# Causal attention in a Mamba-2/MLA decoder trunk: score banks in pairs, low probabilities side by side, work only behind a tile's last chunk

## The chip, the cores and the metric

The kernel runs on one core of a Trainium2 chip. The metric is the device time of one execution in microseconds. The profile is of one such execution; its engines are PE (TensorE matmuls; PEld are its weight loads), DVE (VectorE), ACT (ScalarE), POOL (GpSimd) and SP (SyncE, which only issues DMAs here).

## The reference

Two layers are computed on 2048 rows of width 1024: a Mamba-2 mixer, then multi-head latent attention with 16 heads, and a final norm. The change lies in the attention alone:

```
for i in range(S // Q_BLOCK):                      # blocks of 128 queries
    s = einsum(q_nope, k_nope) + einsum(q_rope, k_rope)   # 64 + 32 = 96 deep
    mask = (q0 + local)[:, None] >= arange(kv_len)[None, :]
    p = softmax(where(mask, s * scale, -inf))
    outs.append(einsum('bhqk,bkhd->bqhd', p, v[:, :kv_len]))
```

All is float32. The kernel keeps that accuracy by splitting each operand into a high and a low half, so that one product is three matmuls (high by high, high by low, low by high).

## The kernel before, in words

The program is recorded stage by stage: Mamba-2 (`mamba`), the projections of the attention (`mla`), the attention (`attention`, `heads`), and gate, output projection and norm (`back`). PE's order in the attention is the order in which the code is written (`manual_schedule`); on DVE, ACT, POOL and SP a scheduler that works ahead of time fixes the order, and on the chip each engine takes its instructions strictly in it.

`heads` goes through 16 heads, each with four query blocks of 512 (`qb` 0 to 3, called q0 to q3 here), each with four **tiles** of 128 queries (`j` 0 to 3). A tile's scores against its 128 to 2048 keys are computed in **chunks** of up to 512 keys, one PSUM bank each.

For each tile, `scores` does this:

- three matmuls for each chunk (`mm3`, L85 to L87), and in the last chunk one more that adds the causal mask (L1062, or L1060 in the first tile of a head);
- a maximum over each chunk on DVE (L1063, tile `mx`), then the negated maximum over the chunks (L1067, `nm`);
- an exponential of each chunk on ACT (L1075, tile `Pr`), which needs `nm`, sums its row on the way, and is what sets the chunk's bank free; these are recorded between the chunks of the next tile;
- the sum over the chunks on DVE (L1079).

The probabilities then have to be turned, 128 by 128, for the product with the values. A **unit** is one block of 128 keys against a query block. Its turning (`turn`, called T) is up to four transposes on PE into a bank (L1090); ACT then writes the high half as float16 (L123, called the copy here), and DVE subtracts it to get the low half (L124, called the low half). Its product (`values`, called V) is one matmul with the high half and one with the low half (L1100, L1101), both against 128 columns: 64 of the high half of the values, 64 of the low. They add up over the query block in one bank `O`, which `finish` copies out (L1107) and sends to memory.

Scores run about a query block ahead of T and V. How many of these stand behind which chunk is written out by hand in the table `CREDIT`: its entry for block, tile and chunk is a string of T and V, done in that order behind the chunk. For q3 it spreads them over the chunks, such as `("TV", "V", "", "TVTVT")` in the last tile. PSUM has eight banks of 2 KB in a partition: four with the tag `mm` for scores, four with the tag `tr` for the turned blocks and `O`; the first 18 chunks of the stage alternate between both. The buffers `Pr` are 24 of 512 columns.

POOL and SP carry the DMAs of the stage: POOL loads keys, values and queries of the next head and adds the second half of `O` in memory (L1113); SP stores the first half (L1109).

Of the kernel before, what the change touches and what calls it, by code (L numbers as in the profile page):

```python
# [20 lines left out]
P = 128  # L21
# [12 lines left out]
WSP = 6  # L34
AHEAD = 10
UPS = (0, 1, 2, 3, 6, 4, 5)
NP = 24
SZ = 4
EV0 = ['big', 'Xp', 'big', 'Sp', 'wsp']
EV1 = ['big', 'yT', 'Xp', 'big', 'Sp']  # L40
LAG = 20
DEPTH = 2
CREDIT = (
    (("VT",), ("TV",), ("VT",), ("TV",)),
    (("", "VTVT"), ("", "TTVV"), ("", "TTVV"), ("", "TTVV")),
    (("TT", "", "VVTV"), ("TV", "", "VTTV"), ("TV", "", "TTVV"), ("TTV", "", "TVV")),
    (("T", "", "", "VVTTVTV"), ("T", "V", "", "VTTVTV"), ("T", "V", "V", "TVTTV"), ("TV", "V", "", "TVTVT")),
)
MAGIC = 12582912.0
PSCALE = 32768.0  # L50
TINY = 2.0 ** -100
# [17 lines left out]
class Net:  # L69
# [5 lines left out]
    def name(self, s):  # L75
        self.n += 1
        return f"{s}_{self.n}"

    def t(self, pool, tag, shape, dt=F32, bufs=None):
        return pool.tile(shape, dt, name=self.name(tag), tag=tag, bufs=bufs)  # L80


# [234 lines left out]
    def layers(self):  # L317
        with ExitStack() as ctx:
            tc = self.tc
            early = ExitStack()  # L320
# [691 lines left out]
    def attention(self):  # L1012
        with ExitStack() as ctx:
            self.wo = self.tail.enter_context(self.tc.tile_pool(name="wo", bufs=1, side="right", reuse_waits="tile"))
            self.wraw = []
            sp = ctx.enter_context(self.tc.tile_pool(name="asp", bufs=2, reuse_waits="tile"))
            with self.tc.manual_schedule(engines={mybir.EngineType.PE}):
                self.heads(sp)

    def heads(self, sp):  # L1020
        nc, v = self.nc, self.nc.vector
        begun = []
        keys, vals, quer = self.keys, self.vals, self.quer

        def cuts(kv):

            out, at = [], 0
            while at < kv:
                w = min(TB, kv - at)
                if kv - at == TB + P:  # L1030
                    w = 384
                out.append((at, max(w, 256)))
                at += w
            return out

        def scores(h, qb, st):
# [8 lines left out]
            for j in range(4):  # L1045
                qs = slice(j * P, (j + 1) * P)
                parts = cuts(qb * TB + (j + 1) * P)
                nb = len(parts)
                mx = self.t(sp, "mx", [P, 4], bufs=4)
                banks = []  # L1050
                for n, (c0, w) in enumerate(parts):
                    if late:
                        late.pop(0)()
                    begun.append(0)
                    s = self.t(self.pp, "tr" if len(begun) <= 18 and len(begun) % 2 == 1 else "mm", [P, TB], bufs=4)
                    ks = slice(c0, c0 + w)
                    self.mm3(s[:, :w], Q[:, 0, qs], Q[:, 1, qs], K[:, 0, ks], K[:, 1, ks], True, n < nb - 1)
                    if n == nb - 1:
                        if qb == j == 0:
                            nc.tensor.matmul(s[:, 0:w], self.idb, self.mk, start=False, stop=True)  # L1060
                        else:
                            nc.tensor.matmul(s[:, w - P:w], self.idb, self.mk[:, 0:P], start=False, stop=True)  # L1062
                    v.tensor_reduce(mx[:, n:n + 1], s[:, :w], AX.X, ALU.max)  # L1063
# [3 lines left out]
                v.tensor_reduce(nm, mx[:, :nb], AX.X, ALU.max, negate=True)  # L1067
                p = {}
                sm = self.t(sp, "sm", [P, 4], bufs=4)
                st["P"].append(p)  # L1070

                def exp(n, j=j, nb=nb, parts=parts, banks=banks, nm=nm, p=p, sm=sm):
                    s, w = banks[n]
                    x = self.t(sp, "Pr", [P, TB], bufs=NP)
                    nc.scalar.activation(x[:, :w], s[:, :w], AF.Exp, bias=nm, accum_out=sm[:, n:n + 1])  # L1075
                    for c in range(0, w, P):
                        p[(parts[n][0] + c) // P] = x[:, c:c + P]
                    if n == nb - 1:
                        v.tensor_reduce(sums[h][:, 4 * qb + j:4 * qb + j + 1], sm[:, :nb], AX.X, ALU.add)  # L1079

                late += [lambda n=n, f=exp: f(n) for n in range(nb)]
            for f in late:
# [2 lines left out]
        def turn(h, qb, kb, st):  # L1085
# [3 lines left out]
            for j in range(jj, 4):  # L1089
                nc.tensor.transpose(pt[:, j * P:(j + 1) * P], st["P"][j][kb], self.ident)  # L1090
            c = slice(jj * P, TB)
            u = self.t(sp, "PTs", [P, 2, TB], F16, bufs=5)
            self.pair16(u[:, 0, c], u[:, 1, c], pt[:, c], PSCALE)
            return u[:, :, c], c

        def values(h, qb, kb, st, u, c):
            if kb == 0:
                st["O"] = self.t(self.pp, "tr", [P, TB], bufs=4)
            nk = 4 * qb + 4
            nc.tensor.matmul(st["O"][:, c], vals[h][:, kb, :], u[:, 0], start=kb == 0, stop=False)  # L1100
            nc.tensor.matmul(st["O"][:, c], vals[h][:, kb, :], u[:, 1], start=False, stop=kb == nk - 1)  # L1101
            if kb == nk - 1:
                finish(h, qb, st)

        def finish(h, qb, st):
            o = self.t(sp, "Os", [P, TB], bufs=3)
# [18 lines left out]
        states = [{"P": []} for _ in jobs]  # L1125
        sums = {}
        def ahead():
            for n, (h, qb) in enumerate(jobs):
# [5 lines left out]
        held = []  # L1134

        def work(what):

            if what == "T" and units:
                a = units.pop(0)
                held.append((a, turn(*a)))  # L1140
            elif what == "V" and held and (len(held) > DEPTH or not units):
                a, (u, c) = held.pop(0)
                values(*a, u, c)

        step = 0
        for credit in ahead():
            step += 1
            if step > LAG:
                for what in credit:
                    work(what)  # L1150
        while units or held:
            work("T")
            work("V")


    def back(self):
        nc, a, v, hp = self.nc, self.a, self.nc.vector, self.hp
        with ExitStack() as ctx:
            sp = ctx.enter_context(self.tc.tile_pool(name="bsp", bufs=2, reuse_waits="tile"))
            self.sp = sp  # L1160
            us = self.t(self.sm, "us", [P, KD])
            nc.sync.dma_start(us, self.us_d.rearrange("(k p) -> p k", p=P))
# [187 lines left out]
```

## Time and profile before

| what | value |
|---|---|
| runs | 3198.4, 3201.06 and 3201.17 us, median 3201.06 |
| the profiled execution's own time | 3198.45 us |
| its span, from first to last instruction | 3196.7 us |
| granted TensorE clock, mean | 0.997 |
| PE, DVE, ACT, POOL busy | 3098.7, 2371.4, 2016.2, 658.8 us |
| first and last score mask of the attention (L1060, L1062) | 2084.9 and 2988.2 us |

The profile's tables are read like this. A group's row names line, engine, operation, output and input tiles, their shapes and the count; then the busy time, the mean duration of one in ns, and the idle time just before them with what ended it. A row of the timeline gives the start in us from the span's beginning, the duration in us, and in brackets the idle time before and its releaser. Matmuls are pipelined: their durations overlap, so the time that one costs is read from the distance of two starts. A row of stretches gives the bounds, the length, and the busy time of each engine asked for with its instructions in brackets, then the granted clock.

### The profile page before, as it was taken

Reading aid. Unit: us, or ns where it says so; the run is one execution under the profiler, and the core shown is the slowest. Engines: PE = TensorE matmul, PEld = TensorE weight load, DVE = VectorE, ACT = ScalarE, POOL = GpSimd, SP = SyncE. Lnnn points to the kernel's source line nnn. Section 1 sums busy time; section 2 is a strip of 40 time slices with the busy share of each in tenths; the row PEclk is TensorE's granted clock in tenths of the full one; section 3 lists DMA queues with packets and bytes.
Section 4 is the critical chain, followed back from the end, with each engine's and each line's share of the span. In section 5 each row is a group of like instructions: output and inputs, shape, how many; then the busy total and the mean of one; then the engine's idle time right before and its main releaser. Section 6 shows DMA issues by size and latency. Waiting matters only on the chain.

```text
span 3196.7 us, 51296 instructions
## 1 busy us (share of the span) xinstructions
PE 3098.7 (97%) x17735; PEld 2244.6 (70%) x17735; DVE 2371.4 (74%) x4786; ACT 2016.2 (63%) x5027; POOL 658.8 (21%) x927
## 2 busy tenths in 40 slices
PE   8999999999999999999999999999999999999998
PEld 6787654556655566665878888877777777777777
DVE  6888787777666666766766665678888888888675
ACT  7888576665555464555646554477877778778522
POOL 1222232321122211312111211322222122222100
PEclk9999999999999999999999999999999999999999
DMA  5443656554343345534486655843434434444494
GB/s 176 131 128 125 225 190 230 189 183 154 133 166 125 120 143 185 172 120 138 128 273 222 222 191 192 266 111 77 92 79 85 86 77 92 81 97 104 99 274 158
DMA packets 213236, 482.52 MB, mean 151 GB/s; under 512 B 28976, under 2 KB 62768, under 8 KB 211536
## 3 DMA queue, kind: packets, MB, share of 16 engines
q1 hardware_dynamic: 160672, 316.02, 31.2%
q0 software_dynamic: 52304, 163.22, 18.9%
q8 instruction: 140, 2.29, 0.3%
q14 instruction: 120, 0.98, 0.1%
HBM read 347.02 MB, written 132.12 MB: 150 GB/s over the span
## 4 chain that ended last, share of the span: by engine, by line
PE 65%; DVE 8%; ACT 6%; DMA 5%; issue 2%; POOL 1%; SPq 0%; ACTq 0%; DVEq 0%; POOLq 0%
PE mm L85 13%; PE mm L86 12%; PE mm L87 12%; PE tr L1090 6%; PE tr L1100 3%; PE tr L1101 3%; PE tr L86 3%; PE tr L87 3%; PE tr L85 3%; DVE cacc L495 2%; DMA wraw<-in_ssm_w_in_dram 2%; PE tr L699 1%; ACT Pr L1075 1%; DMA os<-ri_d 1%; DMA big<-cumT 1%
## 5 line engine op out<-in xcount | busy, mean ns | idle before, releaser
L124 DVE SCALAR_TENSOR_TENSOR PTs<-tr,PTs 128x512 f16<-128x512 f32 (+3 forms) x640 | 375.0, 607 | 92.4 <-ACT PTs L123 86.6
L123 ACT ACTIVATE PTs<-tr 128x512 f16<-128x512 f32 (+3 forms) x640 | 328.5, 541 | 141.1 <-PE tr L1090 140.7
L1063 DVE TENSOR_REDUCE mx<-mm 128x1 f32<-128x512 f32 (+2 forms) x631 | 375.7, 608 | 46.8 <-PE mm L87 44.3
L1075 ACT ACTIVATE Pr<-mm,nm 128x512 f32<-128x512 f32 (+2 forms) x631 | 395.7, 636 | 23.1 <-DVE nm L1067 21.4
L1090 PE MATMUL tr<-pack,Pr 128*128 128x128 f32 x2176 | 317.6, 273 | 1.4 <-ACT Os L1107 1.3
L85 PE MATMUL mm<-xT,wsp 128*128 128x512 f16 (+1 forms) x800 | 310.3, 388 | 0.0
L85 PE MATMUL mm<-K,xT 96*128 96x512 f32 (+2 forms) x639 | 287.0, 449 | 23.3 <-ACT Pr L1075 21.9
L86 PE MATMUL mm<-xT,wsp 128*128 128x512 f16 (+1 forms) x800 | 307.6, 384 | 0.0
L87 PE MATMUL mm<-xT,wsp 128*128 128x512 f16 (+1 forms) x800 | 307.3, 385 | 0.2 <-DVE wsp L116 0.2
L1090 PEld LDWEIGHTS tr<-pack,Pr 128*128 128x128 f32 x2176 | 253.2, 141 | 49.8 <-ACT Os L1107 2.1
L495 DVE SCALAR_TENSOR_TENSOR cacc<-craw,pack,cacc 128x512 f32<-128x512 f32 x288 | 219.9, 785 | 27.6 <-ACT cacc L493 25.5
L85 PE MATMUL mm<-wsp,xT 128*128 128x512 f16 (+2 forms) x640 | 235.9, 369 | 3.1 <-ACT craw L489 3.0
L86 PE MATMUL mm<-wsp,xT 128*128 128x512 f16 (+2 forms) x640 | 234.2, 366 | 0.0
L87 PE MATMUL mm<-wsp,xT 128*128 128x512 f16 (+2 forms) x640 | 233.6, 366 | 0.0
L86 PE MATMUL mm<-K,xT 96*128 96x512 f32 (+2 forms) x639 | 231.8, 363 | 0.0
L87 PE MATMUL mm<-K,xT 96*128 96x512 f32 (+2 forms) x639 | 231.2, 362 | 0.0
L1100 PE MATMUL tr<-PTs,xT 128*128 128x512 f16 (+3 forms) x640 | 222.2, 349 | 0.1
L1101 PE MATMUL tr<-PTs,xT 128*128 128x512 f16 (+3 forms) x640 | 219.7, 347 | 0.0
L85 PE MATMUL mm<-wsp,yT 128*128 128x512 f32 x512 | 208.9, 408 | 8.4 <-DMA wsp<-wo_d 4.5
L692 ACT ACTIVATE Xw<-tr,d_wend 128x64 f32<-128x64 f32 x512 | 112.0, 329 | 155.8 <-DVE y L689 127.6
L86 PE MATMUL mm<-wsp,yT 128*128 128x512 f32 x512 | 204.1, 399 | 0.0
L87 PE MATMUL mm<-wsp,yT 128*128 128x512 f32 x512 | 203.9, 398 | 0.0
(421 smaller groups left out, 7417.9 us busy)
## 6 DMA issues: line engine op xcount, KB each, us to landing
wsp<-wo_d SPq DMA_DIRECT2D x96, 512.0 KB, 3.6
wraw<-in_ssm_w_in_dram SPq DMA_DIRECT2D x128, 256.0 KB, 3.0
big<-cumT SPq DMA_DIRECT2D x64, 512.0 KB, 4.7
wsp<-w_d SPq DMA_DIRECT2D x64, 512.0 KB, 3.7
wo_d<-wsp POOLq DMA_DIRECT2D x32, 512.0 KB, 4.6
w_d<-wsp POOLq DMA_DIRECT2D x32, 512.0 KB, 5.0
xT<-qn_d POOLq DMA_DIRECT2D x64, 256.0 KB, 4.6
K<-kn_d POOLq DMA_DIRECT2D x15, 1024.0 KB, 8.4
```

Of the source, the lines that this page charges most:

```text
L85: mm(out, l_hi, r_hi, start=start, stop=False)
L86: mm(out, l_hi, r_lo, start=False, stop=False)
L87: mm(out, l_lo, r_hi, start=False, stop=stop)
L123: self.nc.scalar.activation(hi, src, AF.Copy, scale=scale)
L124: self.nc.vector.scalar_tensor_tensor(lo, src, scale, hi, ALU.mult, ALU.subtract)
L495: nc.vector.scalar_tensor_tensor(acc, raw[:, k:k + TB], wk[k], acc, ALU.mult, ALU.add)
L692: act(Xw[:, hc], px[:, hc], AF.Copy, scale=wend[:, h0 + h:h0 + h + 1])
L1063: v.tensor_reduce(mx[:, n:n + 1], s[:, :w], AX.X, ALU.max)
L1075: nc.scalar.activation(x[:, :w], s[:, :w], AF.Exp, bias=nm, accum_out=sm[:, n:n + 1])
L1090: nc.tensor.transpose(pt[:, j * P:(j + 1) * P], st["P"][j][kb], self.ident)
L1100: nc.tensor.matmul(st["O"][:, c], vals[h][:, kb, :], u[:, 0], start=kb == 0, stop=False)
L1101: nc.tensor.matmul(st["O"][:, c], vals[h][:, kb, :], u[:, 1], start=False, stop=kb == nk - 1)
```

## The change

Four things change in the attention.

1. **Scores by pairs of banks.** A tile's keys are cut into pieces of up to 1024 (two chunks of equal width side by side in a pair of banks). There are two such pairs, in a pool of their own; the four `tr` banks stay. One maximum (L1072 in the changed kernel) and one exponential (L1084) take a whole pair, and the first 18 chunks no longer use `tr`. `Pr` becomes 14 buffers of 1024.
2. **All T and V behind the tile's last chunk.** `CREDIT` goes; `BEHIND` gives one string for each query block, done behind the last chunk of each of its tiles.
3. **Low probabilities side by side.** `values` does the high half alone (L1112). The low halves are kept (`PTl`, 18 buffers) until the query block is through; `lows` then multiplies them all in a row (L1123), against the 64 columns of high values only, even units into partitions 0 to 63 of `O` and odd ones into 64 to 127. The product of low probabilities and low values is left out.
4. **A row sum of one piece** is copied by POOL (L1090 of the changed kernel) and not reduced by DVE: 8 of 16 tiles of a head.

```diff
+BEHIND = ("TV", "TVTV", "TTVVTV", "TTVVTVTV")
...
-                out.append((at, max(w, 256)))
+                out.append((at, 1, max(w, 256)) if w <= TB else (at, 2, w // 2))
...
-                for n, (c0, w) in enumerate(parts):
...
-                    s = self.t(self.pp, "tr" if len(begun) <= 18 and len(begun) % 2 == 1 else "mm", [P, TB], bufs=4)
...
-                    v.tensor_reduce(mx[:, n:n + 1], s[:, :w], AX.X, ALU.max)
-                    banks.append((s, w))
-                    yield CREDIT[qb][j][n]
+                for c0, m, w in parts:
+                    for i in range(m):
...
+                        if i == 0:
+                            pair = self.t(self.pm, "pair", [P, 2, TB], bufs=2)
+                            banks.append(pair[:, :m, :w])
...
+                        if i == m - 1:
+                            v.tensor_reduce(mx[:, len(banks) - 1:len(banks)], banks[-1], AX.XY, ALU.max)
+                        yield BEHIND[qb] if end else "", end
                 nm = self.t(sp, "nm", [P, 1], bufs=4)
                 v.tensor_reduce(nm, mx[:, :nb], AX.X, ALU.max, negate=True)
...
-                    nc.scalar.activation(x[:, :w], s[:, :w], AF.Exp, bias=nm, accum_out=sm[:, n:n + 1])
+                    nc.scalar.activation(x.rearrange("p (m w) -> p m w", m=m), banks[n], AF.Exp, bias=nm,
+                                         accum_out=sm[:, n:n + 1])
...
+                        if nb == 1:
+                            nc.gpsimd.tensor_copy(sums[h][:, 4 * qb + j:4 * qb + j + 1], sm[:, 0:1])
...
-            nc.tensor.matmul(st["O"][:, c], vals[h][:, kb, :], u[:, 1], start=False, stop=kb == nk - 1)
+        def lows(h, qb, st):
+            nk = len(st["lo"])
+            for i, (kb, l, c) in enumerate(st["lo"]):
+                d = slice(i % 2 * 64, i % 2 * 64 + 64)
+                nc.tensor.matmul(st["O"][d, c], vals[h][:, kb, 0:64], l, start=False, stop=i >= nk - 2)
+            finish(h, qb, st)
```

What stands in a row is shown at three places of one head (the ninth), with the line numbers of the kernel that the rows are from.

First DVE, at the end of the last tile of q3 and so of the head's scores. The change, from the tile's first maximum to its negated maximum `nm`:

```order
L1072 TENSOR_REDUCE mx_27929<-pair_27932 128x1
L1092 TENSOR_REDUCE sum_27221<-sm_27928 128x1
L1072 TENSOR_REDUCE mx_27929<-pair_27943 128x1
L127 SCALAR_TENSOR_TENSOR PTl_27958<-tr_27952,PTh_27957 128x512
L127 SCALAR_TENSOR_TENSOR PTl_27967<-tr_27961,PTh_27966 128x512
L127 SCALAR_TENSOR_TENSOR PTl_27978<-tr_27972,PTh_27977 128x512
L127 SCALAR_TENSOR_TENSOR PTl_27987<-tr_27982,PTh_27986 128x384
L1076 TENSOR_REDUCE nm_27991<-mx_27929 128x1
```

Before, the same tile:

```order
L1063 TENSOR_REDUCE mx_28140<-mm_28143 128x1
L124 SCALAR_TENSOR_TENSOR PTs_28153<-tr_28148,PTs_28153 128x512
L1063 TENSOR_REDUCE mx_28140<-mm_28160 128x1
L1063 TENSOR_REDUCE mx_28140<-mm_28169 128x1
L1079 TENSOR_REDUCE sum_27421<-sm_28139 128x1
L1063 TENSOR_REDUCE mx_28140<-mm_28177 128x1
L1067 TENSOR_REDUCE nm_28211<-mx_28140 128x1
L124 SCALAR_TENSOR_TENSOR PTs_28188<-tr_28183,PTs_28188 128x512
```

The negated maximum moved from ahead of the low halves to behind four of them, which belong to the T behind this tile's own last chunk. In a head of the changed kernel low halves stand between last maximum and `nm` in nine of 16 tiles: one in the second and fourth tile of q0, two in the second and fourth of q1, three in the second to fourth of q2, two in the second of q3, four in its last. Before it is five tiles, with one or two each: the first and third of q0, the first two of q1, the first of q3.

Then ACT at the same tile. The change, from the last exponential of the tile before to the first of the next head:

```order
L1084 ACTIVATE Pr_27936,sm_27928<-pair_27864,nm_27926 128x896
L126 ACTIVATE PTh_27957<-tr_27952 128x512
L126 ACTIVATE PTh_27966<-tr_27961 128x512
L126 ACTIVATE PTh_27977<-tr_27972 128x512
L126 ACTIVATE PTh_27986<-tr_27982 128x384
L1084 ACTIVATE Pr_27994,sm_27993<-pair_27932,nm_27991 128x1024
L1084 ACTIVATE Pr_27996,sm_27993<-pair_27943,nm_27991 128x1024
```

Before, the same stretch:

```order
L1075 ACTIVATE Pr_28174,sm_28139<-mm_28102,nm_28137 128x384
L123 ACTIVATE PTs_28188<-tr_28183 128x512
L1075 ACTIVATE Pr_28214,sm_28213<-mm_28143,nm_28211 128x512
L123 ACTIVATE PTs_28198<-tr_28193 128x512
L1075 ACTIVATE Pr_28216,sm_28213<-mm_28160,nm_28211 128x512
L123 ACTIVATE PTs_28208<-tr_28203 128x512
L1075 ACTIVATE Pr_28218,sm_28213<-mm_28169,nm_28211 128x512
L1075 ACTIVATE Pr_28220,sm_28213<-mm_28177,nm_28211 128x512
```

Copies and exponentials took turns; now four copies stand ahead of the tile's first exponential.

Last PE, at the end of the first tile of q3. The change, from its mask to the next T: the four low products of the same head's q0 block, 64 columns of weights each.

```order
L1070 MATMUL pair_27729<-mk,idb 128x128
L1123 LDWEIGHTS xT_26703
L1123 MATMUL tr_27656<-PTl_27608,xT_26703 64x512
L1123 LDWEIGHTS xT_26703
L1123 MATMUL tr_27656<-PTl_27616,xT_26703 64x384
L1123 LDWEIGHTS xT_26703
L1123 MATMUL tr_27656<-PTl_27625,xT_26703 64x256
L1123 LDWEIGHTS xT_26703
L1123 MATMUL tr_27656<-PTl_27684,xT_26703 64x128
L1103 MATMUL tr_27746<-pack,Pr_27368 128x128
```

Before, the same place: high and low products of the last two units of that block.

```order
L1062 MATMUL mm_27947<-mk,idb 128x128
L1100 LDWEIGHTS xT_26882
L1100 MATMUL tr_27904<-PTs_27858,xT_26882 128x256
L1101 LDWEIGHTS xT_26882
L1101 MATMUL tr_27904<-PTs_27858,xT_26882 128x256
L1100 LDWEIGHTS xT_26882
L1100 MATMUL tr_27904<-PTs_27863,xT_26882 128x128
L1101 LDWEIGHTS xT_26882
L1101 MATMUL tr_27904<-PTs_27863,xT_26882 128x128
L1090 MATMUL tr_27961<-pack,Pr_27556 128x128
```

The low products left the rows of the high ones and stand together at the end of the query block. Outside the attention no engine's order changes up to the stage's first scores, and the number of DMAs is the same.

More of the change, by code (lines that the diff above doesn't have):

```diff
@@ L36 @@
 UPS = (0, 1, 2, 3, 6, 4, 5)
-NP = 24
+NP = 14
+NL = 18
 SZ = 4
@@ L77, in name, with banks @@
         return f"{s}_{self.n}"
+    def banks(self, ctx):
+        self.pm = ctx.enter_context(self.tc.tile_pool(name="pm", bufs=4, space=PSUM, reuse_waits="tile"))
     def t(self, pool, tag, shape, dt=F32, bufs=None):
+        if tag == "mm":
+            pool = self.pm
         return pool.tile(shape, dt, name=self.name(tag), tag=tag, bufs=bufs)
@@ L319, in layers @@
             tc = self.tc
+            self.banks(ctx)
             early = ExitStack()
@@ L1098, in values @@
                 st["O"] = self.t(self.pp, "tr", [P, TB], bufs=4)
[L1099 to L1103, printed above, removed]
+            nc.tensor.matmul(st["O"][:, c], vals[h][:, kb, :], u[0], start=kb == 0, stop=False)
+            st["lo"].append((kb, u[1], c))
+            if kb == 4 * qb + 3:
+                owed.append((h, qb, st))
+        def lows(h, qb, st):
[4 more added lines that the diff above has]
+            finish(h, qb, st)
         def finish(h, qb, st):
@@ L1142, in work @@
                 a, (u, c) = held.pop(0)
+                if a[2] == 0 and owed:
+                    lows(*owed.pop())
                 values(*a, u, c)
         step = 0
-        for credit in ahead():
+        for credit, end in ahead():
             step += 1
             if step > LAG:
+                if end and owed:
+                    lows(*owed.pop())
                 for what in credit:
@@ L1159, in back @@
             sp = ctx.enter_context(self.tc.tile_pool(name="bsp", bufs=2, reuse_waits="tile"))
+            self.banks(ctx)
             self.sp = sp
```

60 lines of the change are left out of this document (29 added, 31 removed).

## The prediction

> **What bounds the kernel now.** I read the shares of busy time on the page first, then two stretches: one head of the attention (from one first-tile mask to the next), and the opening of the attention. Columns of a stretch: bounds, length, busy PE, PEld, DVE, ACT, POOL with instructions, clock, DMA share, GB/s. The row of the first-tile mask gives the head's period.
>
> ```profile
> PE 3098.7 (97%) x17735; PEld 2244.6 (70%) x17735; DVE 2371.4 (74%) x4786; ACT 2016.2 (63%) x5027; POOL 658.8 (21%) x927
> 2473.81:2530.86 57.05, 55.77 (x356) 42.83 (x355) 48.07 (x115) 45.27 (x126) 12.07 (x20) 1.00 0.41 84
> 2086.00:2101.00 15.00, 14.05 (x78) 10.81 (x77) 12.99 (x44) 12.06 (x39) 8.13 (x14) 1.00 0.98 199
> L1060 PE MATMUL mm<-mk,idb x15: 283/283/284, 2131.7 to 2931.5; 128*128 128x256 bf16 x15
> ```
>
> PE is the bound: it idles 57.05 - 55.77 = 1.3 us of a head, and (2931.5 - 2131.7) / 14 = 57.1 us is the period throughout. DVE and ACT have 9 and 12 us to spare in a head. So work taken off PE counts in full as long as PE finds no new wait, and every new wait of PE counts in full too. What PE waits for when it does wait is seen in the one long wait of a head, in the second tile of q3 (timeline, DVE, ACT and PE rows picked):
>
> ```profile
> 2508.62 0.23 PE L1062 MATMUL mm<-mk,idb 128*128 128x128 bf16 x1
> ...
> 2509.21 0.88 DVE L1063 TENSOR_REDUCE mx<-mm 128x1 f32<-128x384 f32 x2
> ...
> 2509.72 1.08 ACT L123 ACTIVATE PTs<-tr 128x512 f16<-128x512 f32 x2
> ...
> 2510.35 1.29 DVE L124 SCALAR_TENSOR_TENSOR PTs<-tr,PTs 128x512 f16<-128x512 f32 x2 [0.26 <-ACT PTs L123]
> ...
> 2511.55 0.15 DVE L1067 TENSOR_REDUCE nm<-mx 128x1 f32<-128x4 f32 x1
> ...
> 2511.74 0.69 ACT L1075 ACTIVATE Pr<-mm,nm 128x512 f32<-128x512 f32 x1
> ...
> 2512.57 0.50 PE L85 MATMUL mm<-K,xT 96*128 96x512 f32 x1 [1.21 <-ACT Pr L1075]
> ```
>
> The chain runs: last score, maxima, two low halves, negated maximum, exponential, next score. This is one of the tiles where two low halves stand ahead of `nm`, and PE stands 1.21 us. `nm` ends 0.04 us before the exponential starts, and the score starts 0.14 us after the exponential ends (2511.74 + 0.69 = 2512.43). I use these two lags below. Two copies start 1.08 - 0.60 = 0.48 us apart, two low halves 1.29 - 0.69 = 0.60.
>
> **What PE saves.** The low products go from 128 columns of weights to 64, two at a time. Starts of PE rows give what each step costs now:
>
> ```profile
> 2903.30 0.39 PE L86 MATMUL mm<-K,xT 96*128 96x512 f32 x1
> 2903.53 0.40 PE L87 MATMUL mm<-K,xT 96*128 96x512 f32 x1
> 2903.76 0.23 PE L1062 MATMUL mm<-mk,idb 128*128 128x128 bf16 x1
> 2903.83 0.61 PE L1090 MATMUL tr<-pack,Pr 128*128 128x128 f32 x4
> 2904.27 0.38 PE L1100 MATMUL tr<-PTs,xT 128*128 128x512 f16 x1
> 2904.49 0.38 PE L1101 MATMUL tr<-PTs,xT 128*128 128x512 f16 x1
> 2904.71 0.33 PE L1100 MATMUL tr<-PTs,xT 128*128 128x384 f16 x1
> 2904.87 0.33 PE L1101 MATMUL tr<-PTs,xT 128*128 128x384 f16 x1
> ```
>
> A score matmul costs 0.23 us for 512 columns (0.69 for a chunk), the mask 0.07, a T 0.44 (0.11 for each transpose), a product 0.22 for 512 columns, 0.16 for 384, and so about 0.11 and 0.06 for 256 and 128. A head has 28 low products of 512 and four each of 384, 256 and 128: 28 x 0.22 + 4 x 0.33 = 7.5 us. If two halves of the array really run at once, a query block costs its even units alone, 4.0 us in a head: **3.5 us saved**. The trace has matmuls of 64 columns into two halves, at L699 (two groups with the mean of one in ns, then rows of the timeline):
>
> ```profile
> L668 PE MATMUL tr<-BC,BC 128*128 128x128 f32 x128 | 24.7, 275 | 0.0
> L699 PE MATMUL tr<-Xd,big 128*64 128x64 f32 x2048 | 73.8, 225 | 11.2 <-DVE big L678 7.4 <-DVE Xd L686 2.9 <-issue 0.8
> ...
> 801.97 0.39 PE L668 MATMUL tr<-BC,BC 128*128 128x128 f32 x2
> ...
> 85.46 0.40 PE L87 MATMUL mm<-xT,wsp 128*128 128x512 f32 x1
> 85.78 1.15 PE L699 MATMUL tr<-Xd,big 128*64 128x64 f32 x32
> 86.86 0.50 PE L85 MATMUL mm<-xT,wsp 128*128 128x512 f32 x1
> 87.20 0.39 PE L86 MATMUL mm<-xT,wsp 128*128 128x512 f32 x1
> ```
>
> 32 rows take 1.15 us; less 0.225 for the last, 31 steps of 0.03 us. Full-width rows of 128 columns at L668 stand 0.115 apart (0.39 less 0.275), so serial ones of 64 columns would stand 0.06 apart: they do overlap. That is float32 and short; for long float16 rows the saving lies between 0 and 3.5 us, and I take 3.5. Going in and out of the halves is not free: L699 starts 0.32 us after its forerunner instead of 0.23, and L85 behind it starts 0.12 late and is followed 0.34 later instead of 0.23, together 0.31 us. Four query blocks make 1.2 us. PE's work in a head: 55.8 - 3.5 + 1.2 = **53.5 us**. The other parts move little on PE: the same chunks, masks and transposes.
>
> **What the pairs cost.** Groups over the attention, with the mean of one in ns:
>
> ```profile
> L1075 ACT ACTIVATE Pr<-mm,nm 128x512 f32<-128x512 f32 x392 | 268.9, 695 | 16.8 <-DVE nm L1067 15.2
> L1075 ACT ACTIVATE Pr<-mm,nm 128x256 f32<-128x256 f32 x122 | 60.9, 499 | 0.0
> L123 ACT ACTIVATE PTs<-tr 128x512 f16<-128x512 f32 x440 | 253.7, 600 | 85.8 <-PE tr L1090 85.3
> L1063 DVE TENSOR_REDUCE mx<-mm 128x1 f32<-128x512 f32 x390 | 265.7, 686 | 45.6 <-PE mm L87 43.7 <-PE mm L1062 0.3
> L1063 DVE TENSOR_REDUCE mx<-mm 128x1 f32<-128x256 f32 x122 | 50.7, 415 | 0.3 <-PE mm L1062 0.3
> L124 DVE SCALAR_TENSOR_TENSOR PTs<-tr,PTs 128x512 f16<-128x512 f32 x440 | 294.9, 688 | 75.2 <-ACT PTs L123 69.5
> L124 DVE SCALAR_TENSOR_TENSOR PTs<-tr,PTs 128x384 f16<-128x384 f32 x63 | 34.8, 553 | 2.5 <-ACT PTs L123 2.3
> L124 DVE SCALAR_TENSOR_TENSOR PTs<-tr,PTs 128x128 f16<-128x128 f32 x63 | 17.9, 283 | 4.1 <-ACT PTs L123 4.1
> ```
>
> No row shows a pair. From 256 to 512 columns a maximum gains 0.27 us and an exponential 0.20, so 1024 columns cost 0.69 + 2 x 0.27 = 1.23 and 0.70 + 2 x 0.20 = 1.09 us. Both cost at least what one bank does (0.69 and 0.70); I take the slopes. DVE and ACT issue fewer instructions and gain some us in a head, but neither is the bound, so that gives nothing. POOL's copies of row sums cost nothing as long as POOL, busy 12 of 57 us, is at most four tiles late: only then would an exponential wait for the buffer. `O` lives on until the low products are through, and so do the values; with one bank for it three are left for T, as now, and the next values have most of a head to arrive: nothing for both, but a T that waits for a bank would show it.
>
> In q2 and q3 a tile now fills both pairs, so its first exponential must end before the next tile may start, and it needs the maximum of the second pair, which ends last. PE meanwhile has only the T and V of `BEHIND`. Time from the end of the tile's mask:
>
> - *Last tile of q3* (two pairs of 1024). Second maximum 0.04 to 1.27. PE runs four T and four V with 15 transposes: 15 x 0.11 + 4 x 0.22 = 2.5 us. The fourth T ends at about 2.5, its copy at 3.0; DVE's four low halves end at 3.7, `nm` at 3.75, the exponential runs 3.8 to 4.9, the next score starts at 5.0. **Wait 2.5**, and 0.2 for the second pair.
> - *Last tile of q2* (1024 and 512). Second maximum, behind the first, until 1.1; low halves of 128, 512, 512 (the third copy lands at 2.0) until 2.7; `nm` 2.8; exponential to 3.9; score at 4.1. PE's work: nine transposes 1.0, V of 384, 256 and 128 0.3: 1.3 us. **Wait 2.8**.
> - *Second tile of q2* (1024 and 256). Maximum until 1.2, low halves of 384, 256, 128 until 2.2, `nm` 2.3, exponential to 3.4, score at 3.6; PE's work 6 x 0.11 + 3 x 0.22 = 1.3. **Wait 2.2**.
> - *Last tile of q1* (one pair, two low halves ahead): its exponential ends at 3.8; PE has 1.3 of T and V and one pair of 1.2. **Wait 1.4**.
> - In the same way: first tile of q2 0.8, third (where 16 low products cover much) 0.8; first three of q3 0.6, 1.3, 0.7, in part because copies stand ahead of the exponential on ACT; q0 0.5 in all.
>
> The sum is 2.7 + 2.8 + 2.2 + 1.4 + 0.8 + 0.8 + 0.6 + 1.3 + 0.7 + 0.5 = **13.8 us** in a head. The period becomes 53.5 + 13.8 = 67.3, 10.2 us more than 57.1; over 15 heads (the last one's tail has less behind it) 153 us. The opening has no T and V to cover anything and only two pairs, where eight banks kept PE busy 14.05 of 15 us: 11 tiles, at an estimated 0.7 us (the middle of the shorter waits above), 8 us.
>
> **The clock.** Long waits cost twice here. Stretches of 3.41 us laid on one grid, PE alone (length, busy, clock):
>
> ```profile
> 1590.72:1594.13 3.41, 1.62 (x15) 1.00 0.33 108
> 1594.13:1597.55 3.42, 3.42 (x19) 1.00 0.24 81
> 2109.55:2112.96 3.41, 1.49 (x9) 1.00 0.29 50
> 2112.96:2116.37 3.41, 3.41 (x10) 0.50 0.17 29
> ```
>
> An idle 1.79 us of a stretch left the clock alone; 1.92 us halved it for the next. The waits of 2.2 to 2.8 us fall into one stretch for at least 1.85 us in some two cases of three, twice in a head, 31 times in all; at most 1.7 us each, of which a part falls into the next wait: 1.3 us, **40 us**.
>
> Sum: the profiled execution took 3198.45 us, 2.6 below the median of 3201.06. 3198 + 153 + 8 + 40 = 3399, so against the median about **3400 us**.
>
> **Rivals.**
>
> - *The clock stays up.* The same waits, no halving: 3360. For it: 1.79 us of idle went free, and a wait that the grid cuts in two does too. Against: the halving shown followed 1.92 us, and the longest waits are well above. Chance 0.17. The Trainium skill ("TensorE: Matmul & The Clock Gate", section "Why this matters for your kernels") asks only that PE have no idle gap over about 3 us between bursts. By that rule none of these waits would touch the clock; the trace disagrees, with 1.92 us of 3.41.
> - *The halves do not overlap* for 512 columns: 3.5 us a head more, 56 in all: 3456. The change then doesn't do what its third part says. Against it stand the L699 rows. Chance 0.15.
> - *PE stays covered*, the other side. If DVE and ACT get through a pair well before PE is through `BEHIND`, PE keeps its 1.3 us of waits and a head takes 54.8: 3198 - 16 x 2.3 = 3161. It decides below 57.1 - 53.5 = 3.6 us of waits in a head. For it: DVE and ACT have room. Against: at the last tile of q2 PE has 1.3 us of work against a maximum and an exponential of at least 0.7 each, even with nothing ahead of `nm`. Chance 0.08.
>
> **How the numbers follow.** The forecast has 0.58, the rivals 0.17, 0.15 and 0.08, no change 0.02. If a pair cost what one bank does, most waits would lose 0.39 us and the two behind full pairs 0.93, some 5 of the 13.8: 75 us less, and 20 of the clock's 40: 3305; the low end is a little below, 3290. No overlap and 1.7 us for every halving give 3400 + 56 + 12, the high end 3470. That range leaves out about 2 in 10. Slower by over 0.2% (about what a measurement of this kernel can tell): 0.90, faster 0.08, same 0.02.
>
> **What would show it.** The head's period near 67 us; PE idle of 13 to 14 us in a head, released by the exponential, with the longest waits behind the last tiles of q2 and q3; a maximum of 1024 near 1.23 us and an exponential near 1.09; low products of 512 columns 0.11 us apart on average; about 30 stretches at half clock. A period below 57 us, or idle released by another line (POOL, or T waiting for a bank), would make the prediction wrong.

## The result, and the profile after

The changed kernel takes 3462.74 us (median of four runs, 3458.87 to 3469.60) against 3201.11 us: 1.082 of the time before, with a 95% interval of 1.0807 to 1.0834. The forecast was 3400 us in a range of 3290 to 3470. The profiled execution took 3463.57 us.

First the row of the first-tile mask of the changed kernel, which gives the head's period, as L1060 did before:

```profile
L1068 PE MATMUL pair<-mk,idb x16: 283/284/437, 2090.9 to 3178.8; 128*128 128x256 bf16 x16
```

Then stretches of it: the first head, the 14 heads behind it, one head, and the opening. Columns: bounds, length, busy PE, PEld, DVE, ACT, POOL with instructions, clock, DMA share, GB/s.

```profile
2090.91:2164.84 73.93, 57.66 (x246) 42.19 (x244) 37.00 (x69) 32.90 (x71) 14.69 (x31) 0.75 0.27 63
2164.84:3178.85 1014.01, 856.37 (x4945) 624.23 (x4943) 647.73 (x1258) 609.93 (x1307) 196.98 (x376) 0.93 0.33 70
2310.07:2382.36 72.29, 61.47 (x354) 44.92 (x354) 46.51 (x90) 43.47 (x94) 13.47 (x27) 0.92 0.30 65
2090.91:2105.91 15.00, 12.92 (x45) 9.85 (x44) 6.60 (x15) 5.44 (x14) 7.51 (x18) 0.63 0.64 150
```

The same 14 heads of the kernel before (PE alone, then clock, DMA share, GB/s):

```profile
2131.72:2931.53 799.81, 781.00 (x4944) 1.00 0.44 89
```

The period went from 799.81 / 14 = 57.13 to 1014.01 / 14 = 72.43 us. PE idles (1014.01 - 856.37) / 14 = 11.26 us of a head instead of 1.34. Its busy time rose too, from 55.79 to 61.17, with as many instructions (of which the low products are narrower): the clock is 0.93 instead of 1.00. From first to last mask the span grew by 241.3 us, of which 214.2 are these 14 heads and 27.1 the first one; the last head brings 18 more. The first mask also comes 6 us later, but that is not the change: two kernels below whose code up to there is that of before have it at 2090.8 and 2089.7.

What PE waits for, over the 14 heads (us in total, times, longest):

```profile
PE pair L88 <- ACT Pr L1084: 153.3, 109, 5.0
PE tr L1103 <- DVE PTl L127: 0.7, 3, 0.3
```

Only the exponential counts; POOL's copies and the bank of `O` cost nothing. The single wait of 5.0 us is a case of its own: in the fifteenth head a step of the next stage on ACT (L1200), which waits for a DMA, stands ahead of the exponential. One such wait, behind the last tile of q2 (timeline, rows of all engines picked):

```profile
2347.93 1.82 DVE L1072 TENSOR_REDUCE mx<-pair 128x1 f32<-128x1024 f32 x2 [0.38 <-PE pair L90]
...
2348.41 0.23 PE L1070 MATMUL pair<-mk,idb 128*128 128x128 bf16 x1
...
2349.67 1.65 DVE L127 SCALAR_TENSOR_TENSOR PTl<-tr,PTh 128x128 f16<-128x128 f32 x3
2349.74 0.22 PE L1112 MATMUL tr<-PTh,xT 128*128 128x128 f16 x1
2351.24 0.14 DVE L1076 TENSOR_REDUCE nm<-mx 128x1 f32<-128x2 f32 x1
...
2351.48 1.11 ACT L1084 ACTIVATE Pr<-pair,nm 128x1024 f32<-128x1024 f32 x1 [0.88 <-DVE nm L1076]
...
2352.74 0.50 PE L88 MATMUL pair<-K,xT 96*128 96x512 f32 x1 [2.77 <-ACT Pr L1084]
```

PE issues its last product at 2349.74. Then come three low halves, `nm`, and 1.11 us of exponential, for which ACT stood 0.88 us idle: PE stands 2.77 us. By tile, the mean waits of a head are 1.4 behind the last tile of q1; 0.7, 2.3, 0.3 and 2.9 behind the four of q2 (2.8 without the one of 5.0); 0.0, 0.9, 0.3 and 2.1 behind those of q3.

What these waits do to the clock is seen in stretches of 3.41 us on the grid on which it changes (length, PE busy, clock, DMA share, GB/s):

```profile
2422.58:2426.00 3.42, 0.65 (x4) 1.00 0.26 29
2426.00:2429.41 3.41, 3.41 (x12) 0.50 0.65 125
2470.37:2473.78 3.41, 2.02 (x13) 1.00 0.71 153
2473.78:2477.20 3.42, 2.72 (x20) 1.00 0.10 23
2494.26:2497.68 3.42, 1.19 (x5) 1.00 0.41 65
2497.68:2501.09 3.41, 3.41 (x15) 0.50 0.33 88
2501.09:2504.50 3.41, 3.41 (x15) 0.50 0.17 38
```

After 2.77 us of idle the next stretch runs at half clock, after 1.39 it doesn't, and after 2.23 it does for two stretches, though PE was busy throughout the first. Over the 15 heads from 2164 us on the clock fell 35 times for 45 stretches. Of the 34 stretches at full clock with 1.78 us of idle or more, 33 were followed by half clock (the other had 1.78); of those with less only two, with 1.68 and 1.40. By tile, the last of q2 was followed by a fall in all 15 heads, the second of q2 in 13, the last of q3 in only four; three falls came behind other tiles. This is not chance from head to head: from 2412 us on, nine of the ten distances between the falls behind the second tile of q2 are 71.68 us, 21 stretches, so the waits keep their place on the grid. In all, 215.2 us ran at half clock, where it was 20.8 before.

### The profile page after: what moved, and what is told of

The parts are those of the page before. It is cut to its first block, busy times and chain, and to the rows that moved or that the text cites. A ratio compares the mean times of both kernels' runs of the same rounds, so it can differ in the third digit from the quotient of the medians.

```text
span 3461.7 us, 50588 instructions
## 1 busy us (share of the span) xinstructions
PE 3197.7 (92%) x17735; PEld 2282.5 (66%) x17735; DVE 2346.1 (68%) x4402; ACT 1983.2 (57%) x4515; POOL 683.1 (20%) x1055
## 4 chain that ended last, share of the span: by engine, by line
PE 55%; DVE 14%; ACT 9%; DMA 5%; issue 4%; POOL 1%; SPq 0%; ACTq 0%; DVEq 0%; POOLq 0%
PE mm L88 8%; PE mm L90 8%; PE mm L89 8%; PE pair L88 5%; PE tr L1103 4%; DVE PTl L127 4%; PE pair L90 3%; PE pair L89 3%; ACT Pr L1084 3%; PE tr L89 3%; PE tr L90 3%; PE tr L88 3%; DVE mx L1072 3%; ACT PTh L126 2%; DVE cacc L499 2%
## 5 line engine op out<-in xcount | busy, mean ns | idle before, releaser
L127 DVE SCALAR_TENSOR_TENSOR PTl<-tr,PTh 128x512 f16<-128x512 f32 (+3 forms) x640 | 366.6, 605 | 161.0 <-ACT PTh L126 159.2
L126 ACT ACTIVATE PTh<-tr 128x512 f16<-128x512 f32 (+3 forms) x640 | 322.5, 534 | 243.7 <-PE tr L1103 235.8
L88 PE MATMUL pair<-K,xT 96*128 96x512 f32 (+4 forms) x640 | 287.4, 449 | 186.3 <-ACT Pr L1084 182.6
L1072 DVE TENSOR_REDUCE mx<-pair 128x1 f32<-128x1024 f32 (+6 forms) x384 | 347.7, 916 | 158.0 <-PE pair L90 71.9
L1084 ACT ACTIVATE Pr<-pair,nm 128x1024 f32<-128x1024 f32 (+6 forms) x384 | 334.0, 871 | 119.6 <-DVE nm L1076 114.7
L1103 PE MATMUL tr<-pack,Pr 128*128 128x128 f32 x2176 | 353.0, 291 | 3.3 <-DVE PTl L127 1.4
L88 PEld LDWEIGHTS pair<-K,xT 96*128 96x128 f32 x640 | 131.8, 206 | 279.2 <-ACT Pr L1084 260.1
L1103 PEld LDWEIGHTS tr<-pack,Pr 128*128 128x128 f32 x2176 | 265.4, 150 | 69.2 <-DVE PTl L127 26.0
L90 PE MATMUL pair<-K,xT 96*128 96x512 f32 (+4 forms) x640 | 253.1, 396 | 0.0
L89 PE MATMUL pair<-K,xT 96*128 96x512 f32 (+4 forms) x640 | 250.1, 391 | 0.0
L1112 PE MATMUL tr<-PTh,xT 128*128 128x512 f16 (+3 forms) x640 | 208.3, 359 | 0.4 <-ACT PTh L126 0.3
```

The costliest lines, as they stand in the source:

```text
L88: mm(out, l_hi, r_hi, start=start, stop=False)
L89: mm(out, l_hi, r_lo, start=False, stop=False)
L90: mm(out, l_lo, r_hi, start=False, stop=stop)
L126: self.nc.scalar.activation(hi, src, AF.Copy, scale=scale)
L127: self.nc.vector.scalar_tensor_tensor(lo, src, scale, hi, ALU.mult, ALU.subtract)
L1072: v.tensor_reduce(mx[:, len(banks) - 1:len(banks)], banks[-1], AX.XY, ALU.max)
```

## The experiments

The theory: pairs make one long chain (maximum, low halves, negated maximum, exponential) end in every tile, PE has too little behind it, and the long waits halve the clock. The rivals: the low products in a row cost the time (the halves, or what they covered), or the waits come from the new order of T and V rather than from pairs. All results in one table; "lost" is half of the time at half clock, per head, the most that the clock can have taken. A to E are the changed kernel with the edit named, F to J the kernel before. Each ratio is to runs of the kernel before on the same chip (medians 3200.94 to 3204.34 us).

| kernel | median us | ratio, interval | period | PE busy | PE idle | lost |
|---|---|---|---|---|---|---|
| before | 3201 | 1 | 57.13 | 55.79 | 1.34 | 0.0 |
| changed | 3462.74 | 1.082, 1.0807 to 1.0834 | 72.43 | 61.17 | 11.26 | 4.9 |
| A `nm` early | 3364.08 | 1.0499, 1.0477 to 1.0521 | 65.76 | 58.18 | 7.58 | 1.8 |
| B waits filled | 3406.74 | 1.0646, 1.0624 to 1.0668 | 68.84 | 64.23 | 4.61 | 0.1 |
| C low products as before | 3424.11 | 1.0698, 1.0682 to 1.0714 | 70.18 | 60.89 | 9.29 | 2.7 |
| D A and C | 3337.27 | 1.0423, 1.0408 to 1.0438 | 64.94 | 59.57 | 5.38 | 1.5 |
| E pairs alone | 3516.32 | 1.0984, 1.0967 to 1.1001 | 76.71 | 61.90 | 14.80 | 4.7 |
| F before, T and V behind | 3260.47 | 1.0186, 1.0172 to 1.0201 | 60.91 | 57.72 | 3.18 | 0.9 |
| G before, low side by side | 3272.29 | 1.0220, 1.0205 to 1.0236 | 61.72 | 56.66 | 5.06 | 0.7 |
| H before, low in a row, full width | 3315.12 | 1.0352, 1.0335 to 1.0368 | 64.14 | 58.44 | 5.70 | 0.2 |
| I before, `nm` early | 3197.33 | 0.9984, 0.9975 to 0.9993 | 56.97 | 55.81 | 1.16 | 0.0 |
| J before, first exponential early | 3206.29 | 1.0011, 1.0003 to 1.0020 | 57.42 | 56.06 | 1.36 | 0.0 |

**A. The negated maximum ahead of the low halves.** Recorded right behind the last maximum:

```diff
                         if i == m - 1:
                             v.tensor_reduce(mx[:, len(banks) - 1:len(banks)], banks[-1], AX.XY, ALU.max)
+                        if end:
+                            nm = self.t(sp, "nm", [P, 1], bufs=4)
+                            v.tensor_reduce(nm, mx[:, :nb], AX.X, ALU.max, negate=True)
                         yield BEHIND[qb] if end else "", end
-                nm = self.t(sp, "nm", [P, 1], bufs=4)
-                v.tensor_reduce(nm, mx[:, :nb], AX.X, ALU.max, negate=True)
```

> The changed kernel with one edit: the negated maximum is recorded straight after the tile's last maximum, ahead of T and V. Of low halves at most one stands ahead of it now instead of two to four. If its place on DVE makes the waits: those behind the second and last tile of q2, the last of q3 and the last of q1 shrink by 0.8 to 1.6 us each, some 5 to 6 us of idle PE in a head, hardly any wait reaches 1.85 us any more and most of the half-clock stretches go with them: about 3320 us. If the pairs themselves make the waits (too few banks, a longer maximum and exponential), with DVE's order beside the point: 3440 to 3465 us.

Its waits over 14 heads:

```profile
PE pair L88 <- ACT Pr L1085: 101.8, 115, 2.1
```

No wait is longer than 2.1 us (2.8 in most heads of the change, 5.0 once); the sum falls by a third, and the time by 99 us. The low halves ahead of `nm` are part of the chain, as the theory has it; the gain is smaller than expected (99 us and not 143), and 7.58 us of idle stay. Part of what stays is on ACT: behind the last tiles of q2 and q3, where PE still waits 1.8 and 0.9 us, the exponential now starts right behind a copy, with no idle time of ACT between them. The waits of 0.7 and 0.8 us behind the first tile of q2 and the second of q3 were of this kind before the edit and did not shrink. And the clock still fell 15 times in the 14 heads, after idle times of only 1.53 to 1.79 us in a stretch.

**B. The waits filled with useless work.** Four tiles of a head get 61 more transposes of the unit matrix into a spare bank, which nothing reads:

```diff
+FILL = {(2, 0, 1): 9, (2, 1, 2): 14, (2, 3, 2): 20, (3, 3, 3): 18}
...
+                if fill:
+                    ft = self.t(self.pp, "tr", [P, TB], bufs=4)
+                    for i in range(fill):
+                        nc.tensor.transpose(ft[:, i % 4 * P:(i % 4 + 1) * P], self.ident, self.ident)
```

> The changed kernel with useless transposes of the identity into a free bank, where PE would wait: 9 ahead of the second pair of q2's first tile, 14, 20 and 18 behind the second and last tile of q2 and the last of q3; 61 of 0.11 us in a head, 6.7 us more work, all of it shorter than the wait that it fills. If idle time of more than about 1.85 us in a stretch of the 3.41 us grid halves the clock, most half-clock stretches of the attention go and the kernel gets faster by doing more: 3380 to 3410 us. If the clock does not follow PE's idle time: 3460 us or more.

Its 14 heads, and the same wait as above (PE rows):

```profile
2161.04:3124.80 963.76, 899.18 (x5799) 1.00 0.35 73
```

```profile
2335.83 0.22 PE L1113 MATMUL tr<-PTh,xT 128*128 128x128 f16 x1
2336.09 2.40 PE L1180 MATMUL tr<-pack 128*128 128x128 f32 x20
2338.82 0.50 PE L89 MATMUL pair<-K,xT 96*128 96x512 f32 x1 [0.33 <-ACT Pr L1085]
```

Twenty transposes stand where PE stood for 2.77 us, and 0.33 us are left. By the distances of starts the 61 take 7.6 us of a head, and the kernel is 56 us faster. Idle falls by 11.26 - 4.61 = 6.65 us of a head, so the work costs about 0.9 us of its own, 15 us in all; the time at half clock falls from 215.2 to 68.2 us, half of which is 73.5 us. 73.5 - 15 = 58 is the gain. The measured gain is 56. So a half-clock stretch costs close to half its length, and with more work and less idle the clock falls less often.

**C and D. The low products where they were,** all 128 columns wide, right behind the high ones: part 3 undone. D has A's edit as well.

```diff
             nc.tensor.matmul(st["O"][:, c], vals[h][:, kb, :], u[0], start=kb == 0, stop=False)
-            st["lo"].append((kb, u[1], c))
+            nc.tensor.matmul(st["O"][:, c], vals[h][:, kb, :], u[1], start=False, stop=kb == nk - 1)
```

> The changed kernel without its third part: the low product stands behind the high one again, 128 columns wide. PE gets 2.3 us more work in a head. If PE is bound by the waits behind the last chunk, the work falls into them: idle PE shrinks by about 2 us in a head, some half-clock stretches go, 3430 to 3470 us. If PE's work counted in full: 3500 us. If the narrow products did not overlap or their switching cost more than they save: clearly faster, below 3420 us, with no less idle time.

> The changed kernel with the negated maximum straight behind the last maximum and with full-width low products, so parts one, two and four of the change without late maxima and without part three. If the two gains seen one by one (99 and 39 us) add up, as they do where the low products fill waits that the early maximum leaves: 3310 to 3340 us, idle PE of 5 to 6 us in a head. If they fill the same time: 3350 to 3365 us.

C is 39 us faster than the change with more work on PE (a little below the 3430 expected): the products cover 2 us of idle in a head. With the lost clock taken out, C and the change have the same period (70.18 - 2.68 = 67.50; 72.43 - 4.88 = 67.55); nearly the whole difference is the clock. D lies where it was expected, in time and in idle: the two gains nearly add up (125 us for 99 and 39). It is the fastest with pairs, and still 136 us slower than before.

**E, F, G. Each part alone.** E is the change with the old table `CREDIT` and C's products, so pairs and POOL's copies alone. F is the kernel before with all T and V of a tile behind its last chunk. G is the kernel before with part 3 (without the product of low probabilities and low values, as in the change). Lines of the three edits, E first, then F, then G:

```diff
-                        yield BEHIND[qb] if end else "", end
+                        yield CREDIT[qb][j][n], end
...
-    (("TT", "", "VVTV"), ("TV", "", "VTTV"), ("TV", "", "TTVV"), ("TTV", "", "TVV")),
-    (("T", "", "", "VVTTVTV"), ("T", "V", "", "VTTVTV"), ("T", "V", "V", "TVTTV"), ("TV", "V", "", "TVTVT")),
...
+    (("", "", "TTVVTV"),) * 4,
+    (("", "", "", "TTVVTVTV"),) * 4,
...
+                d = slice(i % 2 * 64, i % 2 * 64 + 64)
+                nc.tensor.matmul(st["O"][d, c], vals[h][:, kb, 0:64], l, start=False, stop=i >= nk - 2)
```

> The changed kernel with pairs (and POOL's copies) alone: T and V spread over the chunks by the table of before, full-width low products. What stands ahead of a pair's second chunk cannot cover the wait for the pair, so less stands behind the last chunk than in the change. If pairs make the waits: idle PE of 9 us or more in a head, 3430 to 3500 us. If the place of T and V made them: under 3300 us.

> The kernel before with the second part alone: all T and V behind a tile's last chunk, in the change's order, with single banks and full-width low products. A single bank is free after a maximum of 0.69 and an exponential of 0.70 us instead of 1.23 and 1.09, and T and V behind the last chunk are longer by the low products. If the waits come from pairs and bare work behind the chunk together: waits of 2 to 3 us in a head, no half-clock stretches, 3210 to 3240 us. If moving the work behind the last chunk is the cause by itself: 3300 us or more.

> The kernel before with the third part of the change alone: narrow low products in a row, banks and order of scores, T and V as before. If two halves overlap and PE stays covered as before: 2.3 us less in a head, about 3165 us. If the products, taken out of the places where they covered the exponentials, turn into waits: 3190 to 3230 us, with idle PE of 3 us or more in a head.

The 14 heads of E, of F and of G (length, PE busy, clock, DMA share, GB/s):

```profile
2161.50:3235.41 1073.91, 866.66 (x4944) 0.94 0.32 66
```

```profile
2134.25:2986.92 852.67, 808.09 (x4944) 0.99 0.39 83
```

```profile
2131.13:2995.16 864.03, 793.23 (x4945) 0.99 0.41 83
```

Pairs alone cost 315 us, more than the whole change and more than expected: they are enough to cause it. Whether it is the longer operations, or that two banks now come free only together, so that two pieces of scores can be under way and not four, no run here tells apart. T and V behind the last chunk cost 59 us on single banks, which lies between the two expectations, and the clock fell there too, which was not expected. Yet together with pairs they gain: C, which is E with them, is 92 us faster than E and has 5.5 us less idle in a head. G, at 71 us slower than before, lies above both of its ranges, with the idle time of the second. Waits come up that the products had covered: 5.06 us of idle in a head instead of 1.34, of which 59.9 us over the 14 heads, of 70.8, end with the exponential.

These runs also show that idle time alone does not tell when the clock falls. One stretch of F and two of E, each with the one behind it:

```profile
2239.12:2242.53 3.41, 2.14 (x11) 1.00 0.16 35
2242.53:2245.94 3.41, 3.41 (x15) 0.50 0.27 37
```

```profile
2873.04:2876.45 3.41, 1.42 (x10) 1.00 0.00 0
2876.45:2879.86 3.41, 3.19 (x19) 1.00 0.00 0
2896.93:2900.34 3.41, 1.39 (x8) 1.00 0.30 41
2900.34:2903.75 3.41, 3.41 (x11) 0.50 0.02 5
```

In F 1.27 us of idle halved the clock seven times in the 14 heads, and twice did not; in D eleven of 12 falls followed 1.06 to 1.13 us, in G four of five followed 1.47. In E 1.99 us went free and 2.02 didn't. Of E's 26 stretches at full clock with 1.73 to 2.02 us of idle half were followed by half clock: those in which PE spent 0.8 us or more on score matmuls. The 13 that went free had at most 0.14 us of them. So what PE does in the rest of a stretch counts too; how, no run here tells apart.

**H. What made G slower.** As G, but each low product of the row against all 128 columns and into all of `O`:

```diff
-                d = slice(i % 2 * 64, i % 2 * 64 + 64)
-                nc.tensor.matmul(st["O"][d, c], vals[h][:, kb, 0:64], l, start=False, stop=i >= nk - 2)
+                nc.tensor.matmul(st["O"][:, c], vals[h][:, kb, :], l, start=False, stop=i == nk - 1)
```

> The kernel before, with the low products kept until their query block is through and then done in a row, as with the low products side by side alone (3272 us, 61.7 us in a head, of it 5.1 idle), but each against all 128 columns and into all of O. It tells apart what made that kernel slower. Theory: the low products had covered PE's waits for turned blocks and exponentials, so putting them off uncovers these: idle of 4 to 5 us in a head, PE's work back at 55.8, a period near 60.5 and some 3250 to 3275 us in all. Rival: the cost lies in the change to half the array and back (four times in a head, what stands behind it shifted too): then nothing changes its width here, idle stays below 2.5 us, the period is 57 to 58.5 and the time 3200 to 3225 us.

Its 14 heads:

```profile
2137.97:3035.93 897.96, 818.18 (x4944) 1.00 0.40 79
```

Putting the products off costs 64.14 - 57.13 = 7.0 us of a head, and doing them side by side gives 64.14 - 61.72 = 2.4 of it back. So the change of width is not the cost; the rival falls. The time, 3315 us, is well above what the theory said too. The idle time is a little above it; PE's busy time is 2.65 us above that of before, which it did not say. Waits have a tail that counts as busy (below), but that all 2.65 us are such tails was not shown.

**I and J. The kernel before with A's edit, and with the first exponential recorded there too.** The waits point to `nm`; so does the one long wait of before.

```diff
                     banks.append((s, w))
+                    if n == nb - 1:
+                        nm = self.t(sp, "nm", [P, 1], bufs=4)
+                        v.tensor_reduce(nm, mx[:, :nb], AX.X, ALU.max, negate=True)
                     yield CREDIT[qb][j][n]
-                nm = self.t(sp, "nm", [P, 1], bufs=4)
-                v.tensor_reduce(nm, mx[:, :nb], AX.X, ALU.max, negate=True)
```

> The kernel before with one edit: the negated maximum straight behind the tile's last maximum. In the first tile of q3 one low half stands ahead of it instead of two. If the 1.2 us wait of each head behind that tile comes from there: 0.6 us less in a head, 3188 to 3196 us, and a kernel faster than both. If it comes from the three copies ahead of the exponential on ACT, which stay: 3199 to 3203 us.

> The kernel before, with each tile's negated maximum and the exponential of its first chunk written ahead of the T and V behind the tile's last chunk, where the negated maximum alone gave 0.9984 of the time and left most of the 1.2 us wait. Theory (two copies that stand ahead of the exponential on ACT are what is left of that wait): if the order of ACT follows, PE's idle falls from 1.2 to about 0.6 us in a head and the time to 3186 to 3194 us. Rival: the copies wait in turn, T find no free bank and low halves come late, so the wait only moves: 3196 to 3215 us.

The waits of PE for the exponential in I, over its 14 heads:

```profile
PE mm L85 <- ACT Pr L1076: 13.7, 15, 1.0
```

The wait of a head shrinks from 1.2 to 1.0 us only, and the time lies between the two expectations. I is the one version below the kernel before, by 0.16%: the interval just leaves out no change, but the gain is too small to build on. J has the same 1.0 us wait and a new short one, and gains nothing; its time lies in its rival's range. What stands between `nm` and the exponential on ACT there was not taken apart further.

## Why the prediction was right, and what was mis-sized

**The bound, and what a pair costs: right.** PE stayed the bound, and its waits end with the exponential. Groups over 14 heads (count, busy, mean of one in ns, idle before them), ACT and DVE:

```profile
L1084 ACT ACTIVATE Pr<-pair,nm 128x1024 f32<-128x1024 f32 x126 | 140.0, 1112 | 55.9 <-DVE nm L1076 55.9
```

```profile
L1072 DVE TENSOR_REDUCE mx<-pair 128x1 f32<-128x1024 f32 x126 | 154.3, 1224 | 67.9 <-PE pair L90 56.9 <-PE pair L1070 10.6
```

The estimates were 1.09 and 1.23 us. In the wait shown above the parts end within 0.2 us of the forecast's: counted from 2348.48, the mask's start and the 0.07 us that it costs, the maxima end at 1.3 (forecast 1.1), the low halves at 2.8 (2.7), the exponential at 4.1 (3.9), and the next score starts at 4.3 (4.1).

**The low products side by side: right in the price, blind to the place.** They are 0.11 us apart, as forecast (PE rows of the changed kernel, all but the first 0.2 us at full clock):

```profile
2343.86 1.90 PE L1123 MATMUL tr<-PTl,xT 128*64 128x512 f16 x16
2345.68 0.28 PE L1140 MATMUL tr<-pack,ri 128*16 128x128 f32 x1
```

(2345.68 - 2343.86) / 16 = 0.114 us, and the net gain of 3.5 - 1.2 = 2.3 us of a head was 2.4 between H and G. The rival that the halves don't overlap falls. But the low products had stood where PE waits, and moving them to the end of the block costs more than their width saves: G and H show it in the kernel before, C in the changed one. The prediction had their loss inside its waits and did not set it against the saving, so it could not say that part 3 is a loss by itself.

**The waits: right in sum.** Forecast 13.8 us in a head, measured 11.26 of idle. I counted from the issue of the last product to that of the score; the trace counts idle from the product's modelled end. In the wait shown the last product is issued at 2349.74 and costs 0.06, so that is 2352.74 - 2349.80 = 2.94 against 2.77, and the score behind it is followed 0.34 instead of 0.23 us later. Taken for every wait (an estimate from this one), these 0.28 us make 2.2 us for 109 / 14 = 7.8 waits of a head that stand in PE's busy time, and 11.26 + 2.2 is 13.5. That the sum is so close is in part luck. The long waits were right, behind q1 and q2 to 0.1 us; that behind the last tile of q3 was put too high (2.7, measured 2.1), the short ones were too (2.6 for the first three tiles of q3, measured 1.2; 0.5 for q0, measured nothing), and the slow first score, which the forecast didn't have, makes up for some of it. With the lost clock taken out, the period is 67.55 us against 67.3 forecast.

**The clock: the mis-sized term.** It was 40 us, from 31 halvings of one stretch at 1.3 us each. The time at half clock grew by 215.2 - 20.8 = 194.4 us, which is 57 stretches; B shows that each costs about half its length, 1.7 us: 97 us. That is 57 us more than forecast, most of the 63 between the forecast's 3400 and the result. Four things went into it.

- The falls were more and lay elsewhere. The forecast let each of three waits of a head be hit two times in three. Those behind the second and last tile of q2 were hit 28 times of 30, that behind the last of q3 four times of 15, and three falls came behind other tiles: 35 and not 31, 7 us.
- Ten of the 35 lasted two stretches: 17 us.
- The part that I let the next wait absorb was not absorbed, since the stretch behind a wait is full of scores: 1.7 and not 1.3 us for each of the 31, 12 us.
- The opening was charged next to none. The first head ran 37.5 us at half clock, of which 27.3 in one piece, where it was 3.4 before; with two stretches more ahead of it that is 12 stretches, 20 us.

The other 6 or 7 us are small: without the clock the 15 heads grew by 155.5 us instead of 153 and the opening by 10 instead of 8, and what stands ahead of the attention by 2.6. The measure itself, idle time from about 1.85 us on, did well in the changed kernel, which was in part luck: in D, E, F and G it does not hold.

**The rival that the clock stays up** falls with the same rows: waits of under 3 us halve it. In the changed kernel 1.78 us of idle in one stretch of the grid was enough in 33 of 34 cases, and B gains 56 us by filling such waits. The Trainium skill ("TensorE: Matmul & The Clock Gate", section "Why this matters for your kernels") asks for no idle gap of PE over about 3 us and so would see no danger in a wait of 2.8 us; these runs disagree.

**The rival that PE stays covered** needed less than 3.6 us of waits in a head. No version with pairs came near: D, with both remedies, has 5.38 (B's 4.61 is bought with 7.6 us of useless work).

## What to carry to other kernels

Merging banks to halve the number of operations lengthens the chain that sets a bank free, and where PE is the bound and lives on few banks, that chain is what costs: ask first what PE does between the last score of a pair and its exponential. Work that looks removable may be what covers a wait; price the place before the work. Waits of PE of one to three microseconds can cost twice, once for themselves and once for the half clock behind them, at half of each stretch that follows: look at the granted clock stretch by stretch.

## What was not expected of the hardware

- More work made the kernel faster: 61 useless transposes in a head took 56 us off, and the time saved is that of the half clock.
- The half clock sometimes stays for a second stretch (10 of 35 cases). In seven of the ten PE was busy throughout the first, to 0.02 us; in the other three it idled 0.1 to 0.6 us. What decides that stays open.
- No one idle time in a stretch of 3.41 us decides. In the first two kernels the border lies near 1.8 us: before, 1.79 went free and 1.92 didn't; after, 1.78 once went free and once didn't. Two halvings after 1.68 and 1.40 don't fit and stay unexplained. Elsewhere 1.06 us (D) and 1.27 (F) were enough, and 1.99 (E) was not.
